# Attention scores: the lower half of the queries against 64 rows of keys, without a copy of that half

## The chip, the cores and the metric

The kernel runs on one core of a Trainium2 chip. The metric is the device time of one execution, in microseconds (us); the time given for a kernel is the median of its runs.

## What is computed

The reference is a trunk of two layers over 2048 tokens of width 1024. A layer normalises its input, multiplies it with `w_in` into eight sections, and runs two mixers beside each other: chunked softmax attention with 8 heads of width 64, and retention with 4 heads of width 128. Both are gated, joined, multiplied with `w_out` and added to the input. What the change touches is the attention's scores:

```python
qc = q.astype(jnp.float32).reshape(b, nc, CHUNK, h, dh)
...
kb = jnp.concatenate([kp[:, j:j + nc] for j in range(LEFT_CHUNKS + 1)], axis=2)
...
scores = jnp.einsum("bnqhd,bnkhd->bnhqk", qc, kb) * (dh ** -0.5)
...
scores = jnp.where(valid, scores + bias[None, None], NEG_INF)
p = jax.nn.softmax(scores, axis=-1)
```

A chunk of queries sees its own chunk of keys and the 8 before it.

## The kernel before, in words

All large products are made of f16 numbers that are split in two: an upper half (the f32 number rounded to f16) and a lower half (what is left, again in f16). A product of two split numbers takes three matmuls: upper by upper, upper by lower, lower by upper. The sums are kept in f32.

The work of a layer is tiled into four head groups (s), each with two attention heads and one retention head, and within a group into four stages (n) of 512 tokens. A stage has two dense parts and one attention part. `dense_T` (L654) makes queries, keys and the retention's rotated rows with channels on the partitions; `dense_V` (L785) makes values and gates with tokens on the partitions. `attention` (L823) works on the stage that was made before: 8 units of 128 queries and one head each, and beside it `retention` (L909). The order of the work on TensorE, ScalarE, VectorE and GpSimd is written out by hand as one program order: `run` (L1219) lets the dense generator go on for one round (8 matmuls of 512 columns as a rule), then gives the attention generator its turn, then some background work, while `later` (L637) puts small steps off by a number of rounds. A unit takes three rounds: `qk` (L830) with the scores in the first, the products with values (`pv`, L860) a unit or two later. The DMAs are issued from SyncE's queue (SP); those wrapped in `in_turn` keep their place in the program order, the others are placed by the framework's scheduler.

How the scores are stored and made before the change:

- In `evacuate(0)` (L673 to L689) the 512 query columns of both heads leave PSUM with 64 channels of each head on 64 partitions. ScalarE writes the upper half into `qq[:, 0]` (L677), one round later VectorE writes the lower half into `qq[:, 1]` (L680), and one round after that four DMAs (L687) copy both halves into `st.q`, so that for each head `hx` its 64 rows stand twice, on partitions 0 to 63 and again on 64 to 127.
- In `evacuate(1)` (L690 to L703) the keys go to `st.k[:, hx]`: 64 rows hold the upper half and the other 64 rows the lower half. For head 0 the upper half is on partitions 0 to 63, for head 1 on 64 to 127.
- In `qk` one matmul over 128 rows therefore makes q times the upper plus q times the lower half of the keys. The keys of a unit are up to 640 columns, cut into pieces (`cuts`, L840) where a new stage of keys or a new PSUM bank begins. Each piece gets two matmuls directly behind each other: the upper half of q (L845) and the lower half (L846). The 1184 products load their own weights, 128 columns of queries.
- VectorE adds the bias and takes the maximum (L849), ScalarE takes the exponential (L852) and its upper half (L854), GpSimd the lower half (L855), and a DMA transposes both (L857) for `pv` (L865 to L867).

Other lines that the prediction names: L778 and L797 are the dense products, L899 those of the retention, L1172 those of `w_out`. L581 and L587 belong to `rel_reverse` (L567), which turns the bias table round once at the start with small f32 products of 16 rows or 16 columns of weights; L272 are f32 transposes of the input, L761 dense products of the first stage, L1318 a product with ones that sums over partitions. The q copies of the first stage run before the first unit.

Of the kernel before, what the change touches and what calls it, by code (L numbers as in the profile page):

```python
# [8 lines left out]
F16 = mybir.dt.float16  # L9
# [3 lines left out]
AF = mybir.ActivationFunctionType  # L13
ALU = mybir.AluOpType
# [4 lines left out]
P = 128  # L19
# [8 lines left out]
def hybrid_trunk(ctx: ExitStack, tc: tile.TileContext, x, pos, gain, gcol, w_in, w_out, rel, fgain,  # L28
# [8 lines left out]
    act, dve, pool, pe, sp = nc.scalar, nc.vector, nc.gpsimd, nc.tensor, nc.sync  # L37
# [4 lines left out]
    b1 = ctx.enter_context(tc.tile_pool(name="b1", bufs=1))  # L42
    b2 = ctx.enter_context(tc.tile_pool(name="b2", bufs=2))
# [579 lines left out]
    def in_turn(i):  # L623

        if not ring.get("free"):
            return
        tc.keep_in_program_order(i)
# [9 lines left out]
    def later(k, fn):  # L637
        deferred.append([k, fn])
# [11 lines left out]
    def in_order(apart, terms):  # L650

        return [(kt, w) for w in terms for kt in range(KT)] if apart else [(kt, w) for kt in range(KT) for w in terms]

    def dense_T(l, s, n, g, st):  # L654
        hh, hl = hT[l, n]
        nm = f"{l}_{s}_{n}"
        st.tabc = b1.tile([P, 512], F32, tag="tabc", name=f"tabc{nm}")
        st.tabs = b1.tile([P, 512], F32, tag="tabs", name=f"tabs{nm}")
        def tab_load():
            while n not in tab_done:  # L660
                pull(1)
            in_turn(sp.dma_start(st.tabc, tab_d[n][0]))
            in_turn(sp.dma_start(st.tabs, tab_d[n][1]))

        first = (l, s, n) == (0, 0, 0)

        def soon(fn):
            if first:
                fn()
            else:  # L670
                later(1, fn)

        def evacuate(j, ps):  # L673
            if j == 0:
                st.q = b2.tile([P, 2, 2, 512], F16, tag="q", name=f"q{nm}")
                qq = b1.tile([P, 2, 512], F16, tag="qq", name=f"qq{nm}")
                act.activation(qq[:, 0, :], ps, AF.Copy, scale=2.0 ** -16)  # L677

                def q_rest():
                    dve.scalar_tensor_tensor(out=qq[:, 1, :], in0=ps, scalar=2.0 ** -16, in1=qq[:, 0, :], op0=ALU.mult,  # L680
                                             op1=ALU.subtract)
                    soon(q_copies)

                def q_copies():
                    for hx in range(2):
                        for half in range(2):
                            in_turn(sp.dma_start(st.q[half * 64:half * 64 + 64, hx], qq[hx * 64:hx * 64 + 64]))  # L687

                soon(q_rest)  # L689
            elif j == 1:  # L690
                st.k = b3.tile([P, 2, 512], F16, tag="k", name=f"k{nm}")
                kk = b1.tile([P, 2, 512], F16, tag="swp", name=f"kk{nm}")
                kh, kl = kk[:, 0, :], kk[:, 1, :]
                act.activation(kh, ps, AF.Copy, scale=2.0 ** -16)

                def k_rest():
                    dve.scalar_tensor_tensor(out=kl, in0=ps, scalar=2.0 ** -16, in1=kh, op0=ALU.mult, op1=ALU.subtract)  # L697
                    sp.dma_start(st.k[0:64, 0, :], kh[0:64, :])
                    sp.dma_start(st.k[64:128, 1, :], kh[64:128, :])
                    sp.dma_start(st.k[64:128, 0, :], kl[0:64, :])  # L700
                    sp.dma_start(st.k[0:64, 1, :], kl[64:128, :])

                soon(k_rest)  # L703
            else:
                w = 5 - j
                rot = b2.tile([P, w, 512], F16, tag=f"rot{j}", name=f"rot{nm}_{j}")
                if j == 2:
                    raw = rot[:, 1:3].rearrange("p a c -> p (a c)").bitcast(F32)
                else:
                    raw = b1.tile([P, 512], F32, tag="qq", name=f"raw{nm}")  # L710
                act.activation(raw, ps, AF.Copy, scale=2.0 ** -16)

                def swap(rot=rot, raw=raw, j=j):
                    swp = b1.tile([P, 512], F32, tag="swp", name=f"swp{nm}_{j}")
                    sp.dma_start(swp[0:64, :], raw[64:128, :])
                    sp.dma_start(swp[64:128, :], raw[0:64, :])

                    def turn():
                        pool.tensor_tensor(raw, raw, st.tabc, op=ALU.mult)  # L719
                        pool.tensor_tensor(swp, swp, st.tabs, op=ALU.mult)  # L720
                        pool.tensor_tensor(raw, raw, swp, op=ALU.add)  # L721

                    def upper():
                        act.activation(rot[:, 0], raw, AF.Copy)

                    def lower():
                        dve.tensor_tensor(rot[:, 1], raw, rot[:, 0], op=ALU.subtract)

                    def third():
                        act.activation(rot[:, 2], rot[:, 0], AF.Copy, scale=2.0 ** -11)  # L730

                    def tokens():
                        st.kt = b1.tile([P, KT, P], F16, tag="ktok", name=f"kt{nm}")
                        sp.dma_start_transpose(out=st.kt, in_=rot.rearrange("p a c -> p (a c)"))

                    if not first:
                        plan = {3: turn, 6: upper, 7: lower, **({9: third} if j == 2 else {10: tokens})}
                    elif j == 2:
                        plan = {4: turn, 11: upper, 12: lower, 13: third}
                    else:  # L740
                        plan = {3: turn, 5: upper, 6: lower, 7: tokens}
                    for k_, fn in plan.items():
                        later(k_, fn)

                if j == 2:
                    st.rq = rot
                    swap()
                    if first:
                        later(1, tab_load)
                else:  # L750
                    st.rk = rot
                    later(9 if first else 3, swap)

        if first:
            ps = [psD.tile([P, 512], F32, tag="dense", name=f"dT{nm}_{j}") for j in range(2)]
            for (j, a) in ((0, 0), (0, 1), (0, 2), (1, 0), (1, 1), (1, 2), (0, 3), (1, 3)):
                cs = slice(a * P, (a + 1) * P)
                m = 0
                for (w_, h_) in ((g.h, hh), (g.h, hl), (g.l, hh)):
                    for kt in range(KT):  # L760
                        pe.matmul(ps[j][:, cs], w_[:, j, kt, :], h_[:, kt, cs], start=(m == 0), stop=(m == 23))  # L761
                        m += 1
                yield
            for j in range(2):
                evacuate(j, ps[j])
                yield
        for j in range(2 if first else 0, 4):
            if j == 2 and not first:
                tab_load()
            if first:  # L770
                ps = psR.tile([P, 512], F32, tag="small", name=f"dT{nm}_{j}")
            else:
                ps = psD.tile([P, 512], F32, tag="dense", name=f"dT{nm}_{j}")
            while g.tdone <= j:
                pull(1)
            m = 0
            for kt, (w_, h_) in in_order(j == 0, ((g.h, hh), (g.l, hh), (g.h, hl))):
                pe.matmul(ps, w_[:, j, kt, :], h_[:, kt, :], start=(m == 0), stop=(m == 23))  # L778
                m += 1
                if m in (8, 16) or (m == 24 and first):  # L780
                    yield
            evacuate(j, ps)
            yield
# [39 lines left out]
    def attention(l, s, n, g, st, prev):  # L823
# [6 lines left out]
        def qk(a, hx):  # L830
# [7 lines left out]
            S = psS.tile([P, 1024], F32, tag="S", name=f"S{u.nm}")  # L838
            cs = slice(a * P, (a + 1) * P)
            cuts = sorted({0, nb} | {j for j in range(nb) if u.kts[j] == (st, 0) or j == 4})  # L840
            for j0, j1 in zip(cuts, cuts[1:]):
                q_, a_ = u.kts[j0]
                k_ = q_.k[:, hx, a_ * P:(a_ + j1 - j0) * P]
                o = S[:, j0 * P:j1 * P]
                pe.matmul(o, st.q[:, hx, 0, cs], k_, start=True, stop=False)  # L845
                pe.matmul(o, st.q[:, hx, 1, cs], k_, start=False, stop=True)  # L846
            v = b2.tile([P, 640], F32, tag="sc", name=f"sc{u.nm}")[:, 0:w]
            m = b2.tile([P, 1], F32, tag="mq", name=f"mq{u.nm}")
            dve.tensor_tensor_reduce(out=v, in0=S[:, 0:w], in1=g.bias[hx][:, 640 - w:640], scale=1.0, scalar=-3.0e38,  # L849
                                     op0=ALU.add, op1=ALU.max, accum_out=m)  # L850
# [505 lines left out]
    for j in range(4):  # L1356
        o = VSEC[j] * 512
# [80 lines left out]
    for l in range(DEPTH):  # L1438
        gO = [Grp(), Grp()]
        go = Grp()  # L1440
        for s in range(NSW):
            g = grp(l, s)
            for n in range(NS):
                first = (l, s, n) == (0, 0, 0)
                if not first:
                    st = St()
                    states[l, s, n] = st
                    dT = dense_T(l, s, n, g, st)
                else:
                    st = st0  # L1450
# [129 lines left out]
```

## Time and profile before

| what | value |
|---|---|
| median of 3 runs | 2060.21 us (2058.85 to 2062.08) |
| span of the profiled execution | 2060.7 us |
| TensorE products busy | 1999.4 us, 14038 products |
| weight loads busy | 1052.9 us, 14038 loads |
| VectorE, ScalarE, GpSimd busy | 1228.1, 1134.8, 688.1 us |
| mean granted TensorE clock | 0.995 |
| DMA | 313.64 MB, queue busy for 65.6% of 16 engines' span |

The span runs from the first to the last instruction of one profiled execution; the profile lists no time of its own for that execution, and its span lies within the range of the three runs. Engines are named PE (TensorE products), PEld (TensorE weight loads), DVE (VectorE), ACT (ScalarE), POOL (GpSimd) and SP. A row of a group reads: line, engine, operation, tiles written and read, for products the rows and columns of the weights (128*128), shapes, count, then busy time and mean length of one in ns, then the idle time ahead of it and what ended it. A row of the order of time reads: start, length, engine, line, operation, tiles, shapes, how many were merged. The ends of products are modelled and run past the start of the next product, so starts are what is to be compared.

### The profile page before, as it was taken

The numbers are of one execution on the slowest core, as the hardware profiler recorded it, in microseconds if no ns is written. First come the engines' busy times: TensorE is split into PE (matmuls) and PEld (weight loads), VectorE is DVE, ScalarE is ACT, GpSimd is POOL, SyncE is SP. The second block draws the span as 40 slices with busy tenths as digits, with TensorE's granted clock in tenths as the row PEclk, the third lists the DMA queues.
The fourth block names the chain that finished last, engine by engine and source line by source line (L and its number), as shares of the span: only waits on it lengthen the run. The fifth ranks groups of instructions, "written<-read, shape, count | busy, mean of one in ns | idle before, by whom it ended". The sixth has DMA issues, their size and how long they took to land. (4 is left out here: it accounts for less than half of the span.)

```text
span 2060.7 us, 39339 instructions
## 1 busy us (share of the span) xinstructions
PE 1999.4 (97%) x14038; PEld 1052.9 (51%) x14038; DVE 1228.1 (60%) x3804; ACT 1134.8 (55%) x2526; POOL 688.1 (33%) x701
## 2 busy tenths in 40 slices
PE   6988999999999999999999999999999999999998
PEld 4444555555555555554444555555555555555544
DVE  6776666565556555666553556555655566557643
ACT  6556665556565645555444546655656565455432
POOL 0344343434334434430003443444333334333100
PEclk9999999999999999999999999999999999999999
DMA  8778664547584754899774546554746775658864
GB/s 227 169 161 178 155 148 109 112 114 164 117 185 113 165 128 101 174 209 263 219 185 113 124 104 156 116 126 103 158 117 150 148 155 124 129 115 187 224 203 139
DMA packets 645701, 313.64 MB, mean 152 GB/s; under 512 B 459232, under 2 KB 602080, under 8 KB 645504
## 3 DMA queue, kind: packets, MB, share of 16 engines
q1 hardware_dynamic: 645504, 311.12, 65.6%
q8 instruction: 110, 1.80, 0.4%
q14 instruction: 87, 0.71, 0.1%
HBM read 123.26 MB, written 41.98 MB: 80 GB/s over the span
## 5 line engine op out<-in xcount | busy, mean ns | idle before, releaser
L855 POOL TENSOR_TENSOR pq<-sc,pq 128x640 f16<-128x640 f32 (+4 forms) x256 | 319.4, 1248 | 860.5 <-ACT pq L854 443.8
L852 ACT ACTIVATE sc<-sc,mq,cT 128x640 f32<-128x640 f32 (+4 forms) x256 | 218.4, 853 | 615.6 <-DVE rl L871 309.7
L797 PE MATMUL dV<-whV,hTh 128*128 128x512 f16 x1024 | 353.9, 381 | 7.3 <-DVE gt L815 6.1
L797 PE MATMUL dV<-whV,hTl 128*128 128x512 f16 x1024 | 353.8, 381 | 0.0
L797 PE MATMUL dV<-wlV,hTh 128*128 128x512 f16 x1024 | 353.8, 381 | 0.0
L778 PE MATMUL dT<-hTh,whT 128*128 128x512 f16 x1008 | 346.6, 379 | 2.7 <-DVE kk L697 1.3
L778 PE MATMUL dT<-hTl,whT 128*128 128x512 f16 x1008 | 346.6, 379 | 0.0
L778 PE MATMUL dT<-hTh,wlT 128*128 128x512 f16 x1008 | 346.6, 379 | 0.0
L797 PEld LDWEIGHTS <-hTh 128*128 128x128 f16 x2048 | 197.0, 98 | 224.7 <-DVE gt L815 10.0
L778 PEld LDWEIGHTS <-whT 128*128 128x128 f16 x2016 | 192.1, 98 | 207.7 <-issue 1.6
L849 DVE CUSTOM_DVE_ANT_0 sc<-S,bias 128x640 f32<-128x640 f32 (+4 forms) x256 | 188.3, 735 | 88.8 <-PE S L846 87.4
L1172 PE MATMUL dO<-whO,yly 128*128 128x512 f16 x504 | 191.0, 379 | 1.7 <-DMA yly<-hTl 1.1
L1172 PE MATMUL dO<-whO,yhy 128*128 128x512 f16 x504 | 191.0, 379 | 1.0 <-DMA yhy<-hTh 1.0
L1172 PE MATMUL dO<-wlO,yhy 128*128 128x512 f16 x504 | 191.0, 379 | 0.0
L854 ACT ACTIVATE pq<-sc 128x640 f16<-128x640 f32 (+4 forms) x256 | 171.5, 670 | 8.1
L797 PEld LDWEIGHTS <-hTl 128*128 128x128 f16 x1024 | 99.4, 98 | 112.4 <-issue 3.9
L1172 PEld LDWEIGHTS <-yhy 128*128 128x128 f16 x1008 | 98.1, 98 | 113.7 <-DMA yhy<-hTh 1.5
L778 PEld LDWEIGHTS <-wlT 128*128 128x128 f16 x1008 | 97.2, 98 | 113.7 <-issue 6.0
L845 PE MATMUL S<-k,q 128*128 128x128 f16 (+3 forms) x592 | 142.4, 267 | 0.0
L865 PE MATMUL o<-v,pT 128*128 128x65 f16 x1120 | 129.8, 193 | 6.4 <-DMA pT<-pq 5.5
L866 PE MATMUL o<-v,pT 128*128 128x64 f16 x1120 | 130.1, 195 | 0.0
L846 PE MATMUL S<-k,q 128*128 128x128 f16 (+3 forms) x592 | 129.7, 267 | 0.0
(359 smaller groups left out, 3476.5 us busy)
## 6 DMA issues: line engine op xcount, KB each, us to landing
q<-qq SPq DMA_DIRECT2D x128, 128.0 KB, 2.4
yyy<-y_d SPq DMA_DIRECT2D x32, 512.0 KB, 4.5
stT<-in_w_in_dram SPq DMA_DIRECT2D x27, 512.0 KB, 4.8
stV<-in_w_in_dram SPq DMA_DIRECT2D x26, 512.0 KB, 4.6
k<-kk SPq DMA_DIRECT2D x128, 64.0 KB, 2.0
swp<-rot SPq DMA_DIRECT2D x64, 128.0 KB, 3.1
tabc<-tab SPq DMA_DIRECT2D x32, 256.0 KB, 3.0
tabs<-tab SPq DMA_DIRECT2D x32, 256.0 KB, 3.1
```

Source lines behind the costliest of these rows:

```text
L778: pe.matmul(ps, w_[:, j, kt, :], h_[:, kt, :], start=(m == 0), stop=(m == 23))
L797: pe.matmul(ps, h_[:, kt, a * P:(a + 1) * P], w_[:, kt, :], start=(m == 0), stop=(m == 23))
L845: pe.matmul(o, st.q[:, hx, 0, cs], k_, start=True, stop=False)
L846: pe.matmul(o, st.q[:, hx, 1, cs], k_, start=False, stop=True)
L849: dve.tensor_tensor_reduce(out=v, in0=S[:, 0:w], in1=g.bias[hx][:, 640 - w:640], scale=1.0, scalar=-3.0e38, op0=ALU.add, op1=ALU.max, accu ...
L852: act.activation(v, v, AF.Exp, bias=m[:, 0:1], scale=g.c[:, 0:1])
L854: act.activation(pq[:, 0:w], v, AF.Copy)
L855: pool.tensor_tensor(pq[:, w:2 * w], v, pq[:, 0:w], op=ALU.subtract)
L865: pe.matmul(o[:, 0:65], u.p[:, b, :], v_[:, 0:65], start=(b == 0), stop=False)
L866: pe.matmul(o[:, 0:64], u.p[:, b, :], v_[:, 65:129], start=False, stop=False)
L1172: pe.matmul(ps, h_[:, kt, :], w_[:, kt, :], start=(m == 0), stop=(m == 23))
```

## The change

The lower half of q is no longer copied. `st.q` becomes `[P, 3, 512]`: parts 0 and 1 hold the upper half for head 0 and 1, each twice over the partitions as before; VectorE writes the lower half of both heads directly into part 2, where each head has its own 64 rows only. `qq` keeps the upper half alone, and each of the four copies moves one half instead of two. In `qk` all upper products of a unit are issued first, piece by piece, over 128 rows; then all lower products, over the 64 rows where that head's upper half of the keys stands. Products of the lower half of q with the lower half of k are thereby left out of the scores. The first product into a PSUM bank opens it, the last one into it closes it.

```diff
-                st.q = b2.tile([P, 2, 2, 512], F16, tag="q", name=f"q{nm}")
-                qq = b1.tile([P, 2, 512], F16, tag="qq", name=f"qq{nm}")
-                act.activation(qq[:, 0, :], ps, AF.Copy, scale=2.0 ** -16)
+                st.q = b2.tile([P, 3, 512], F16, tag="q", name=f"q{nm}")
+                qq = b1.tile([P, 512], F16, tag="qq", name=f"qq{nm}")
+                act.activation(qq, ps, AF.Copy, scale=2.0 ** -16)
...
-                    dve.scalar_tensor_tensor(out=qq[:, 1, :], in0=ps, scalar=2.0 ** -16, in1=qq[:, 0, :], op0=ALU.mult,
+                    dve.scalar_tensor_tensor(out=st.q[:, 2, :], in0=ps, scalar=2.0 ** -16, in1=qq, op0=ALU.mult,
                                              op1=ALU.subtract)
...
-                            in_turn(sp.dma_start(st.q[half * 64:half * 64 + 64, hx], qq[hx * 64:hx * 64 + 64]))
+                            in_turn(sp.dma_start(st.q[half * 64:half * 64 + 64, hx, :], qq[hx * 64:hx * 64 + 64, :]))
...
             cuts = sorted({0, nb} | {j for j in range(nb) if u.kts[j] == (st, 0) or j == 4})
+            rows = slice(hx * 64, hx * 64 + 64)
+            parts = []
             for j0, j1 in zip(cuts, cuts[1:]):
                 q_, a_ = u.kts[j0]
-                k_ = q_.k[:, hx, a_ * P:(a_ + j1 - j0) * P]
-                o = S[:, j0 * P:j1 * P]
-                pe.matmul(o, st.q[:, hx, 0, cs], k_, start=True, stop=False)
-                pe.matmul(o, st.q[:, hx, 1, cs], k_, start=False, stop=True)
+                parts.append((S[:, j0 * P:j1 * P], q_.k[:, hx, a_ * P:(a_ + j1 - j0) * P]))
+            opened = set()
+            for (j0, (o, k_)) in zip(cuts, parts):
+                pe.matmul(o, st.q[:, hx, cs], k_, start=j0 // 4 not in opened, stop=False)
+                opened.add(j0 // 4)
+            for i, (j0, (o, k_)) in enumerate(zip(cuts, parts)):
+                pe.matmul(o, st.q[rows, 2, cs], k_[rows], start=False,
+                          stop=i + 1 == len(parts) or cuts[i + 1] // 4 != j0 // 4)
```

In the changed kernel's numbering the upper products are L848 and the lower ones L851.

## Prediction

> **What bounds the kernel now.** I read the head of the page first, then the grouped rows, then the order of time inside one attention unit, and last the list of what TensorE waits for.
>
> ```profile
> span 2060.7 us, 39339 instructions
> ...
> PE 1999.4 (97%) x14038; PEld 1052.9 (51%) x14038; DVE 1228.1 (60%) x3804; ACT 1134.8 (55%) x2526; POOL 688.1 (33%) x701
> ...
> L849 DVE CUSTOM_DVE_ANT_0 sc<-S,bias 128x640 f32<-128x640 f32 (+4 forms) x256 | 188.3, 735 | 88.8 <-PE S L846 87.4
> ...
> L846 PE MATMUL S<-k,q 128*128 128x128 f16 (+3 forms) x592 | 129.7, 267 | 0.0
> ```
>
> TensorE is busy for 97% of the span, and no other engine passes 60%. The softmax row counts 256 units (a unit is 128 queries of one head). The score row counts 592 pieces, 592/256 = 2.3 to a unit, each with an upper product (L845) and a lower one (L846), and has no idle time before it. But a product's row runs on past the start of the next one, so what a product costs is the step from its start to the next start. That is read in the order of time (columns: start us, length us):
>
> ```profile
> 620.25 0.38 PE L846 MATMUL S<-k,q 128*128 128x512 f16 x1
> 620.47 0.22 PE L845 MATMUL S<-k,q 128*128 128x128 f16 x1
> 620.52 0.22 PE L846 MATMUL S<-k,q 128*128 128x128 f16 x1
> 620.58 0.38 PE L778 MATMUL dT<-hTl,whT 128*128 128x512 f16 x1
> ```
>
> Steps: 0.22 us for 512 columns, 0.055 us for 128, also from the unit into the dense product behind it. Only columns are paid for. The weight loads show why:
>
> ```profile
> 620.47 0.10 PEld L846 LDWEIGHTS <-q 128*128 128x128 f16 x1
> 620.52 0.15 PEld L778 LDWEIGHTS <-whT 128*128 128x128 f16 x2
> ```
>
> Each load begins with the product ahead of it (620.47, 620.52) and so lies beside that product. The kernel is bound by TensorE's stream, and time is lost or won where a step between starts grows or shrinks.
>
> **The change part by part.**
>
> *Columns: nothing.* The built program has the same 592 + 592 products over the same columns. The lower ones take weights of 64 rows by 128 columns, at row 0 or row 64 by head, in place of 128 by 128. The steps above go by columns, so I give half the rows no saving; the product of the two lower halves is left out of the scores without a gain in time.
>
> *Two changes of shape per unit: the cost.* A unit's products are regrouped: first all upper ones (128 rows), then all lower ones (64 rows), and behind them work on 128 rows again. That is 2 changes of the weights' shape in each of 256 units, 512 in all. The kernel before has four in the whole program, all in the preparation of rel_bias at 27 to 31 us, and they are the nearest rows there are. Merged rows of the products first (start, length of the whole row, count), then single ones, then the loads:
>
> ```profile
> 26.76 0.61 PE L761 MATMUL dT<-hTh,wlT 128*128 128x128 f16 x8
> 27.30 0.54 PE L581 MATMUL rlt<-ident,rl 16*128 16x16 f32 x6
> ...
> 28.29 1.07 PE L272 MATMUL ptn<-ident,xb 128*128 128x128 f32 x8
> 29.30 1.48 PE L587 MATMUL rlr<-anti,rt 128*16 128x128 f32 x12
> ...
> 27.63 0.21 PE L581 MATMUL rlt<-ident,rl 16*128 16x16 f32 x1
> ...
> 30.51 0.27 PE L587 MATMUL rlr<-anti,rt 128*16 128x128 f32 x1
> 30.71 0.23 PE L761 MATMUL dT<-hTh,whT 128*128 128x128 f16 x1
> ...
> 30.71 0.29 PE L761 MATMUL dT<-hTh,whT 128*128 128x128 f16 x2
> ```
> ```profile
> 27.30 0.44 PEld L581 LDWEIGHTS rlt<-ident,rl 16*128 16x128 f32 x6
> 27.77 0.10 PEld L1318 LDWEIGHTS <-ones 128*128 128x128 bf16 x1
> ...
> 29.29 1.20 PEld L587 LDWEIGHTS rlr<-anti,rt 128*16 128x16 f32 x12 [0.17 <-issue]
> 30.71 0.90 PEld L761 LDWEIGHTS <-whT 128*128 128x128 f16 x16 [0.21 <-ACT hTh L281]
> ```
>
> The last start in a merged row is its start plus its length, less the length of one product.
> - From 128*128 to 16*128 weights: last L761 start 26.76 + 0.61 - 0.22 = 27.15, next product 27.30. The step is 0.15, where these products step by (27.15 - 26.76)/7 = 0.055: 0.095 more. The load no longer begins with the product ahead (27.15) but at 27.30, with its own. I read it as the array being emptied first.
> - From 128*128 to 128*16: last L272 start 28.29 + 1.07 - 0.27 = 29.09, next 29.30. The step is 0.21, where the L587 products of the same 128 columns step by (30.51 - 29.30)/11 = 0.11: 0.10 more.
> - Out of 128*16: 30.51 to 30.71, 0.20 in place of 0.11: 0.09 more. The view puts the load's idle time down to ACT, yet the wait is as long as at the other changes.
> - Out of 16*128: the load stands 0.14 behind the last product (27.63 to 27.77); its product then waits for something else. So 0.14 is a bound only.
>
> The first product after a change has no load ahead of it, so the step behind it grows too: after 30.71 the second starts at 30.71 + 0.29 - 0.22 = 30.78, 0.07 in place of 0.055, some 0.01 more.
>
> Per change I take 0.095 + 0.01 = **0.105 us**, between ends of 0.09 and 0.14. No row has 64 rows of weights; the nearest is the first of the four, which also narrows the rows and keeps all columns. For in and out alike, 512 x 0.105 = **53.8 us** (ends 46.1 and 71.7), on the stream that nothing covers.
>
> The Trainium skill, TensorEngine Tiling (Array Packing), Key Properties, says that changing the tiling mode drains the engine, while another tile of the same mode does not; it gives no time. The Trainium skill's TensorE: Matmul & The Clock Gate, Part 2 (the step "DRAIN"), lets the last column leave after about 128 cycles, at 2.4 GHz an estimate from that page of 0.053 us per change, 27 us in all. The rows show nearly twice that, and they decide.
>
> *Stalls that take some of it up.* Where TensorE waits anyway, being later costs less. Of what it waits for from 80 us on (us in total, times, longest), the rows that matter here:
>
> ```profile
> PE r L899 <- DVE dT L907: 6.8, 9, 1.6
> PE o L865 <- DMA pT<-pq: 5.5, 9, 1.9
> ...
> PE dT L778 <- DMA hTh<-xa: 0.8, 1, 0.8
> ...
> PE dT L778 <- DVE qq L680: 0.6, 1, 0.6
> ```
>
> The first and the last are the ends of 15 rows with 37 stalls, 33.8 us. Each stall can hide at most its own length, and at most 2 x 0.105 = 0.21 us for each unit since the stall before; added up stall by stall that is an estimate of 12 us. But the chains that end in dT and pT begin with a product of TensorE and move with it. So 0 to 12, and I take a third: 4 us.
>
> *The copies: nothing on the path.* ScalarE's upper half and VectorE's rest (now written straight into the third part of q) keep their shapes and so their lengths. The built program shows no new wait for them: VectorE's rest even loses its waits for DMAs that read the old tile. On ScalarE, VectorE and GpSimd no instruction changes its place. On SP's queue a handful of issues trade places by one to five with their neighbours: five y_d stores, one load of output weights, one pair of table loads, the two transposes of one token tile. I price these at nothing: the stores have no reader before the output stage, GpSimd (33% busy) reads the tables, and the weights and the token tile are used a stage or more later; a late one would show as a new DMA stall of TensorE. The 128 copies go from 128 to 64 KB:
>
> ```profile
> q<-qq SPq DMA_DIRECT2D x128, 128.0 KB, 2.4
> ...
> k<-kk SPq DMA_DIRECT2D x128, 64.0 KB, 2.0
> ```
>
> By the k row they land 0.4 us sooner. No score product waits for them (idle 0.0). What lighter copies can give is the DMA stalls in layers where they run: 5.5 for pT and 0.8 for hTh, 6.3 us at most. I take 0, because a pT stall follows a chain over VectorE, ScalarE and GpSimd, and its transpose is only the last link.
>
> *Sum.* Against the profiled execution: 2060.7 + 53.8 - 4 = 2110.5 us of span. The median shown (2060.21) lies 0.5 below that span: **2110 us**, 2.4% more.
>
> **The rivals.**
>
> *No emptying at half height, and the lighter copies show (no change or faster).* The place is the step from upper to lower products and back. If 64 rows follow 128 as any other weights do, the time is 2060, and with all 6.3 us of DMA stalls gone 2054. It is faster only if a change of shape costs under 6.3/512 = 0.012 us. For it: no row shows 64 rows. Against it: three changes, in rows and in columns, in and out, read 0.09 or more. Chance 0.08, half of it within 0.2% (4 us, about what a measurement of this kernel can tell from no change) and half faster.
>
> *Loads that no longer lie beside products.* Then the 592 - 256 = 336 lower products that follow a lower one each wait for their load: 0.10 us as at 620.47, or 0.06 at the pace of the six L581 loads. That is 34 or 20 us more, 2130 to 2144. For it: the load of 16*128 at 27.30 did not lie beside the product ahead. Against it: that was only the first; the six products of L581 start within 0.33 us (27.30 to 27.63) with a load each, and the six loads end at 27.74, inside the last product's row. Chance 0.12. The Trainium skill, TensorE: Matmul & The Clock Gate, Part 3, states such a rule: a load overlaps a running product only where their row groups differ. The loads of full height at 620.47 and 620.52 already speak against it.
>
> *A cheap change* (0.05 us): 2060 + 26 = 2086. Against it are the same three readings. Chance 0.03.
>
> **How the numbers follow.** The forecast holds 0.77, with its own ends at 2060 + 46 - 12 = 2094 and 2060 + 72 = 2132. The range of 2094 to 2130 cuts little from it and takes in the edge of the load rival: about 8 in 10. Faster 0.04, same 0.04, slower 0.92 (0.77 + 0.12 + 0.03).
>
> **What would show it.** In the profile after: lower products with 64*128 weights; the step from the last upper product to the first lower one about 0.10 us over its columns, with its load beginning behind that product and not with it; the same from the last lower one to what follows; steps among the lower products by columns alone. TensorE's idle time should hardly grow, because rows of 0.22 us cover steps of 0.16; the span must show it. It would be wrong if the steps across the change stay at 0.055 (first rival), if lower products of 128 columns step by 0.09 or more among themselves (second), or if the span grows where no unit runs.

## The result, and the profile after

The changed kernel takes 2107.41 us (median, 2103.67 to 2107.71), the kernel before 2060.93 beside it: a ratio of 1.0221, 95% interval 1.0207 to 1.0236. It is 46.5 us slower; 2110 us was forecast. The profiled execution took 2107.59 us with a span of 2105.8 us.

The head of the page after, and the row of the softmax's first step:

```profile
span 2105.8 us, 39316 instructions
...
PE 2048.6 (97%) x14038; PEld 1038.7 (49%) x14038; DVE 1228.8 (58%) x3804; ACT 1137.4 (54%) x2526; POOL 690.5 (33%) x701
...
L855 DVE CUSTOM_DVE_ANT_0 sc<-S,bias 128x640 f32<-128x640 f32 (+4 forms) x256 | 188.6, 737 | 117.0 <-PE S L851 115.1
```

The number of products is the same, the busy time of the other engines too. VectorE now sits idle 28 us longer ahead of its softmax step (117.0 against 88.8), nearly all of it waiting for scores: they come later. The page cannot show why TensorE needs longer, because its busy time counts rows that run on past the next start. The groups kept apart by shape say what ran (mean length in ns behind the busy time), lower products first:

```profile
L851 PE MATMUL S<-k,q 64*128 64x128 f16 x304 | 58.6, 218 | 0.0
L848 PE MATMUL S<-k,q 128*128 128x128 f16 x304 | 58.6, 219 | 0.0
```

The rows' lengths are equal and there is no idle time. The order of time in one unit of two pieces shows it, products first, loads second:

```profile
628.08 0.43 PE L848 MATMUL S<-k,q 128*128 128x512 f16 x2
628.45 0.44 PE L851 MATMUL S<-k,q 64*128 64x512 f16 x2
628.82 0.34 PE L905 MATMUL r<-rot,rot 128*128 128x128 f16 x3
```
```profile
628.44 0.11 PEld L851 LDWEIGHTS <-q 64*128 64x128 f16 x2 [0.26 <-issue]
628.82 0.17 PEld L905 LDWEIGHTS <-rot 128*128 128x128 f16 x3 [0.26 <-issue]
```

The last upper product starts at 628.08 + 0.43 - 0.22 = 628.29, the first lower one at 628.45: 0.16 us for 128 columns, which step by 0.055 elsewhere. The last lower one starts at 628.45 + 0.44 - 0.22 = 628.67, the next product at 628.82: 0.15. Both times the load begins with its own product (628.44, 628.82) and not with the one ahead. It is the pattern of the early rows of the kernel before, now twice in every unit. Over all 512 changes of shape in this trace the load starts 4 or 5 ns ahead of its own product, and 0.09 to 0.10 us beyond the columns are spent ahead of both. That the array is being emptied in that time is a reading: the trace shows the wait, not what fills it.

Taken over all starts of products in both traces, the growth of the span divides like this (what a step takes for its columns alone is already taken off in the first four rows):

| where | us |
|---|---|
| from the last upper to the first lower product, 256 x 0.096 | 24.5 |
| from the last lower product to the next work, 255 x 0.095 (one ends in a stall) | 24.3 |
| the product behind that, 256 x 0.011 | 2.8 |
| the second lower product, 192 x 0.011 | 2.0 |
| less what the same steps of the kernel before take over their columns, mostly in stretches of half clock | -0.6 |
| units in all, with the one left out and rounding | 52.7 to 53.3 |
| stalls of TensorE from 80 us on (33.8 before, 28.7 after) | -5.1 |
| what remains, nearly all in stretches of half clock | -2.9 |
| span | 45 |

Two terms give time back. The stalls from 80 us on (us, times, longest):

```profile
PE o L871 <- DMA pT<-pq: 7.8, 7, 2.5
PE dV L797 <- DVE gt L815: 4.1, 3, 3.1
PE r L905 <- DVE sh L913: 3.6, 2, 2.1
PE r L905 <- DVE dT L913: 3.2, 7, 1.1
```

The wait for VectorE's dT fell from 6.8 to 3.2 us, as it would if VectorE, with 0.2 us more per unit, keeps up better; this was not tested by itself. The wait for the transposed pT rose from 5.5 to 7.8, so the lighter copies did not shorten it. The other term is the granted clock (1.00 is full). In the kernel before, then after (stretch, length, products busy, clock, DMA share and GB/s):

```profile
107.40:110.80 3.40, 3.30 (x14) 0.50 0.25 64
121.00:124.40 3.40, 3.23 (x14) 0.50 0.99 309
182.50:189.30 6.80, 5.78 (x31) 0.50 0.55 169
1609.20:1612.60 3.40, 3.40 (x20) 0.51 0.65 181
```
```profile
107.40:110.80 3.40, 3.10 (x25) 1.00 0.24 61
120.70:127.50 6.80, 6.13 (x21) 0.50 1.03 255
182.50:189.30 6.80, 3.75 (x30) 1.00 0.76 201
953.60:957.00 3.40, 3.40 (x10) 0.50 1.19 189
1609.20:1612.60 3.40, 3.40 (x25) 1.00 0.59 134
```

Between the start and the end of the work the kernel before has 17.0 us at half clock, the changed one 10.2. At half clock a step is twice as long (0.43 us for 512 columns at 184 us in the kernel before, 0.22 elsewhere), so 6.8 us less of it is worth up to 3.4 us; the steps say 2.9. The change did not cause this as far as the runs show: the profiled runs below that take as long as the kernel before have 13.7 to 20.5 us of half clock, and the one that takes as long as the changed kernel (the last piece alone over 64 rows) has 17.1. The longest stall of the kernel before (3.3 us, on VectorE's gt) ends at 183.5, inside such a stretch; what starts one was not tried.

### The profile page after: what moved, and what is told of

Same layout as the page of the kernel before. It is cut to its first block, busy times and chain, and to the rows that moved or that the text cites. A ratio compares the mean times of both kernels' runs of the same rounds, so it can differ in the third digit from the quotient of the medians.

```text
span 2105.8 us, 39316 instructions
## 1 busy us (share of the span) xinstructions
PE 2048.6 (97%) x14038; PEld 1038.7 (49%) x14038; DVE 1228.8 (58%) x3804; ACT 1137.4 (54%) x2526; POOL 690.5 (33%) x701
## 4 chain that ended last, share of the span: by engine, by line
PE 51%; DMA 2%; DVE 1%; ACT 1%; POOL 1%; issue 1%; SPq 1%; POOLq 0%; ACTq 0%
PE dO L1178 15%; PE dT L778 14%; PE dV L797 14%; PE r L905 2%; PE S L851 2%; PE S L848 1%; PE o L871 1%; PE o L872 1%; PE o L873 1%; DMA pT<-pq 1%; DMA swp<-rot 0%; DMA stO1m<-in_w_out_dram 0%; ACT sc L858 0%; POOL pq L861 0%; PE ptn L1051 0%
## 5 line engine op out<-in xcount | busy, mean ns | idle before, releaser
L855 DVE CUSTOM_DVE_ANT_0 sc<-S,bias 128x640 f32<-128x640 f32 (+4 forms) x256 | 188.6, 737 | 117.0 <-PE S L851 115.1
L871 PE MATMUL o<-v,pT 128*128 128x65 f16 x1120 | 129.1, 193 | 8.6 <-DMA pT<-pq 7.8
L873 PE MATMUL o<-v,pT 128*128 128x65 f16 x1120 | 128.6, 192 | 0.0
L958 POOL TENSOR_TENSOR rss<-rss,mhalf 128x1 f32<-128x1 f32 x128 | 77.1, 602 | 155.7 <-DVE rss L957 150.5
```

Source lines behind the costliest of these rows:

```text
L871: pe.matmul(o[:, 0:65], u.p[:, b, :], v_[:, 0:65], start=(b == 0), stop=False)
L873: pe.matmul(o[:, 0:65], u.p[:, u.nb + b, :], v_[:, 0:65], start=False, stop=(b == u.nb - 1))
L958: pool.tensor_tensor(ss, ss, mhalf, op=ALU.pow)
```

## The experiments

The theory: the cost is the number of times that the weights' shape changes between 128 and 64 rows (512 of them). Rivals: the products over 64 rows are slow in themselves; the regrouping costs; the data path (direct write, light copies, queue order) costs. Each run stands beside runs of the kernel before on the same chip. "The unit steps" are the steps between starts from a unit's first score product to the second product behind the unit, added up over all units without stalls; a change in them is against the kernel before.

### All products over 128 rows, with zeros

```diff
-                st.q = b2.tile([P, 3, 512], F16, tag="q", name=f"q{nm}")
+                st.q = b2.tile([P, 4, 512], F16, tag="q", name=f"q{nm}")
...
-                    dve.scalar_tensor_tensor(out=st.q[:, 2, :], in0=ps, scalar=2.0 ** -16, in1=qq, op0=ALU.mult,
-                                             op1=ALU.subtract)
+                    for hx in range(2):
+                        r, z = slice(hx * 64, hx * 64 + 64), slice(64 - hx * 64, 128 - hx * 64)
+                        pool.memset(st.q[z, 2 + hx, :], 0.0)
+                        dve.scalar_tensor_tensor(out=st.q[r, 2 + hx, :], in0=ps[r], scalar=2.0 ** -16, in1=qq[r],
+                                                 op0=ALU.mult, op1=ALU.subtract)
...
-                pe.matmul(o, st.q[rows, 2, cs], k_[rows], start=False,
+                pe.matmul(o, st.q[:, 2 + hx, cs], k_, start=False,
```

> The changed kernel with its grouping and its light copies, but each lower product runs over 128 rows again: the lower half of a head has a part of its own, with zeros in the other 64 rows, so the sums are those of the changed kernel (the product of the two lower halves stays out). It adds two GpSimd memsets and a second VectorE instruction per stage. Theory (the cost is the change of the weights' shape, 512 times): no change of shape is left in a unit, every step goes by columns, time back at 2061 (2055 to 2066). Rival (regrouping all upper ahead of all lower products, or the direct write by VectorE, is what costs): it stays near 2107. If the lighter copies are worth anything it would show here as under 2061, by at most 6.

Measured: 2066.11 us, ratio 1.0022 (1.0012 to 1.0032). The unit steps grew by 0.1 us in all, so the 53 us are gone with the shape. Left are 5 us over the kernel before, just past the top of what the theory gave; in the trace TensorE waits 59.1 us in all, 5.2 more than before. The last three experiments below look for them.

### Regrouping alone

```diff
+            parts = []
             for j0, j1 in zip(cuts, cuts[1:]):
...
-                o = S[:, j0 * P:j1 * P]
-                pe.matmul(o, st.q[:, hx, 0, cs], k_, start=True, stop=False)
-                pe.matmul(o, st.q[:, hx, 1, cs], k_, start=False, stop=True)
+                parts.append((S[:, j0 * P:j1 * P], k_))
+            opened = set()
+            for (j0, (o, k_)) in zip(cuts, parts):
+                pe.matmul(o, st.q[:, hx, 0, cs], k_, start=j0 // 4 not in opened, stop=False)
+                opened.add(j0 // 4)
+            for i, (j0, (o, k_)) in enumerate(zip(cuts, parts)):
+                pe.matmul(o, st.q[:, hx, 1, cs], k_, start=False,
+                          stop=i + 1 == len(parts) or cuts[i + 1] // 4 != j0 // 4)
```

> The kernel before with one part of the change alone: all upper products of a unit first, then all lower ones, all over 128 rows, with the double copy. Theory (change of shape): 2061 (2058 to 2064), steps by columns alone. Rival (grouping costs): 2107.

Measured: 2060.15 us, ratio 0.9997 (0.9988 to 1.0006), and 0.0 us of change in the unit steps. The regrouping is free, with its new order of opening and closing the PSUM banks, and that rival falls.

### More changes with the same products

The changed kernel with each lower product directly behind its upper one:

```diff
                 pe.matmul(o, st.q[:, hx, cs], k_, start=j0 // 4 not in opened, stop=False)
                 opened.add(j0 // 4)
-            for i, (j0, (o, k_)) in enumerate(zip(cuts, parts)):
+                i = cuts.index(j0)
                 pe.matmul(o, st.q[rows, 2, cs], k_[rows], start=False,
```

> The changed kernel with the 64-row products where the lower products stood before, each directly behind its upper one. The same 592 lower products of 64 rows, but 1184 changes of shape in place of 512. Theory (each change costs 0.096 us and the product behind it 0.011 more): 1184 x 0.107 = 127 us on the stream, less some 8 to 20 taken up by stalls, so 2168 to 2180. Rival (each product over 64 rows costs, whatever stands ahead of it): no different from 2107.

Measured: 2166.24 us, ratio 1.0510 (1.0495 to 1.0524). One unit of two pieces in its trace:

```profile
643.56 0.38 PE L848 MATMUL S<-k,q 128*128 128x512 f16 x1
643.87 0.39 PE L851 MATMUL S<-k,q 64*128 64x512 f16 x1
644.19 0.23 PE L848 MATMUL S<-k,q 128*128 128x128 f16 x1
644.35 0.23 PE L851 MATMUL S<-k,q 64*128 64x128 f16 x1
644.51 0.23 PE L905 MATMUL r<-rot,rot 128*128 128x128 f16 x1
```

The steps are 0.31, 0.32, 0.16 and 0.16 us in place of 0.22, 0.22, 0.055 and 0.055: 0.1 more at every one of four changes, in and out, behind long and short products. The unit steps grew by 123.3 us, which is 0.104 for each of 1184 changes; in the changed kernel it is 52.7/512 = 0.103. The time came out 2 us under the range that was forecast (2168 to 2180). The stalls gave back 16.0 us (53.9 in the kernel before, 37.9 here), within the 8 to 20 allowed for them; what was sized too high is the stream, 0.104 us for a change in place of 0.107.

### Fewer products over 64 rows, with the same changes

The first experiment with the last lower product of a unit alone over 64 rows:

```diff
-                pe.matmul(o, st.q[:, 2 + hx, cs], k_, start=False,
+                r_ = rows if i + 1 == len(parts) else slice(0, P)
+                pe.matmul(o, st.q[r_, 2 + hx, cs], k_[r_], start=False,
```

> The first experiment with the last lower product of each unit alone over 64 rows, the others over 128 rows with zeros: 256 products of 64 rows in place of 592, but still 512 changes of shape. Theory (changes): 256 x (0.096 + 0.095 + 0.011) = 52 us on the stream, less the 8 that the changed kernel's stalls and slow stretches gave back, so 2103 to 2107. Rival (products over 64 rows): 256/592 of 46.5, 2081.

Measured: 2107.94 us, ratio 1.0229 (1.0215 to 1.0243), with 52.9 us in the unit steps; the time lies 1 us above the range that was forecast (2103 to 2107) and far from the rival's 2081. 256 products over 64 rows cost as much as 592. So it is not their number that counts but that of the changes: this and the run before decide against the rival that 64 rows are slow in themselves.

### The same shape at other rows

```diff
-                pe.matmul(o, st.q[rows, 2, cs], k_[rows], start=False,
+                r_ = slice(64 - hx * 64, 128 - hx * 64) if j0 == 4 else rows
+                pe.matmul(o, st.q[r_, 2, cs], k_[r_], start=False,
```

> The changed kernel, but in the 240 units of five key tiles the last lower product (the one into the second PSUM bank) takes the other 64 rows of q and of the keys: the same 64x128 shape, another place. It computes something else than the scores' term there (the other head's lower half against this head's lower keys). Theory in its narrow form (a change of shape empties the array, a change of place within the shape does not): no step longer than by columns there, 2107, or down to 2094 if products in different rows run beside each other (240 x 0.055). Rival (any change of the rows in use empties the array): 240 x 0.107 = 26 us more on the stream, 2125 to 2133.

Measured: 2098.95 us, ratio 1.0183 (1.0169 to 1.0198). One unit, products and loads:

```profile
888.02 0.43 PE L848 MATMUL S<-k,q 128*128 128x512 f16 x2
888.39 0.39 PE L852 MATMUL S<-k,q 64*128 64x512 f16 x2
888.71 0.23 PE L906 MATMUL r<-rot,rot 128*128 128x128 f16 x1
```
```profile
888.39 0.10 PEld L852 LDWEIGHTS <-q 64*128 64x128 f16 x2 [0.26 <-issue]
```

Two lower products, 512 columns on the one half of the rows and 128 on the other, take 0.39 us together, where they take 0.44 in the changed kernel, and the next work starts 0.32 us after the first of them, not 0.37. Their starts lie 3 ns apart: they run side by side, into different PSUM banks. A change of place within the shape brings no wait, and the rival's 2125 to 2133 falls. In the units of three pieces the product over the other rows starts 6 to 8 ns behind the first lower product, before the second one, although it is issued last (in one unit 256, 128 and 256 columns start at 163.289, 163.296 and 163.409). The unit steps fell from 52.7 to 42.7 us. The units with such a product are 192 and not the 240 of the expectation (the other 64 have a single piece), and 192 x 0.056 = 10.8 us is about what fell away. So it is the shape, in the narrow form of the theory.

### One VectorE write and two more copies

The first experiment, with the lower half going through `qq` and two copies (lines against the changed kernel):

```diff
+                    for hx in range(2):
+                        pool.memset(st.q[64 - hx * 64:128 - hx * 64, 2 + hx, :], 0.0)
+                    dve.scalar_tensor_tensor(out=qq[:, 1, :], in0=ps, scalar=2.0 ** -16, in1=qq[:, 0, :], op0=ALU.mult,
+                                             op1=ALU.subtract)
...
+                        r = slice(hx * 64, hx * 64 + 64)
+                        in_turn(sp.dma_start(st.q[r, 2 + hx, :], qq[r, 1, :]))
```

> The first experiment again (all products over 128 rows, zeros in the other 64 rows), but VectorE writes the lower half in one instruction as in the kernel before, and two more copies of 64 KB per stage bring it to its rows; six copies of 64 KB stand where the kernel before has four of 128. If the 5 us of the first experiment came from the second VectorE instruction per stage: 2061 (2057 to 2063). If they came from the GpSimd memsets or from the tile's zeros: 2066 again. If lighter copies gain anything: under 2058.

Measured: 2064.02 us, ratio 1.0014 (1.0005 to 1.0023). That is between the two answers and its interval overlaps that of the first experiment: inconclusive. It takes VectorE's instruction away, but puts two more issues per stage into SP's queue.

### The slice of rows alone

The changed kernel with one edit:

```diff
-                pe.matmul(o, st.q[rows, 2, cs], k_[rows], start=False,
+                pe.matmul(o, st.q[:, 2, cs], k_, start=False,
```

> The changed kernel with one edit: the lower products take all 128 rows of the third part of q and of the keys, in place of the head's 64. In the other 64 rows that adds the other head's lower half times this head's lower keys, a term of the size of the one that the changed kernel leaves out. Copies, direct write, grouping and queue order are those of the changed kernel; only the shape differs. Theory: 2061 (2056 to 2064), so that the slice of rows alone is the whole difference. If the lighter copies are worth anything: under 2058, to 2054 at best. Rival (something in the data path costs as well, as the 3 to 5 us of the two runs with zero rows may hint): 2063 to 2066.

Measured: 2064.03 us, ratio 1.0010 (1.0001 to 1.0019), with -0.7 us in the unit steps. Two words of the slice are worth 43 us (2107.41 to 2064.03), and the -0.7 is half clock that fell into units of the kernel before. The time lies at the edge of the theory's range and inside the rival's (2063 to 2066), so a small cost in the data path is not excluded. What is left against the kernel before is 0.1%, between 0.2 and 4 us by the interval; the lighter copies and VectorE's lost waits gain nothing that shows. The wait for pT in this run, and VectorE's dT behind it:

```profile
PE o L871 <- DMA pT<-pq: 9.0, 7, 2.6
PE r L905 <- DVE dT L913: 7.8, 11, 1.6
```

Both are longer than before (5.5 and 6.8), with copies of half the size. In the first experiment, with the same copies, the wait for pT is 5.5, so what moves it stays open.

### Two memsets more

The run over full rows, with two GpSimd memsets per stage into a fourth part of `st.q` that nothing reads:

```diff
+                    for hx in range(2):
+                        pool.memset(st.q[hx * 64:hx * 64 + 64, 3, :], 0.0)
```

> The kernel of the run over full rows with two GpSimd memsets of 64x512 per stage into a part of q that nothing reads. If the memsets were what cost in the runs with zero rows: 3 to 5 us over the run over full rows. If not: the same time.

Measured: 2063.14 us, ratio 1.0006 (0.9996 to 1.0015). The memsets cost nothing that can be measured.

### Two VectorE writes in place of one

The run over full rows, with the write split:

```diff
-                    dve.scalar_tensor_tensor(out=st.q[:, 2, :], in0=ps, scalar=2.0 ** -16, in1=qq, op0=ALU.mult,
-                                             op1=ALU.subtract)
+                    for hx in range(2):
+                        r = slice(hx * 64, hx * 64 + 64)
+                        dve.scalar_tensor_tensor(out=st.q[r, 2, :], in0=ps[r], scalar=2.0 ** -16, in1=qq[r],
+                                                 op0=ALU.mult, op1=ALU.subtract)
```

> The kernel of the run over full rows with the lower half written in two VectorE instructions of 64 rows (0.69 us each) in place of one of 128. If VectorE's second instruction was what cost in the first run with zero rows: 3 to 5 us over the run over full rows. If not: the same time.

Measured: 2068.53 us, ratio 1.0027 (1.0016 to 1.0038), 4.5 us over the run over full rows (the intervals just meet). VectorE's rows for the write, in the kernel before and in this one, then what TensorE waits for in this one:

```profile
L680 DVE SCALAR_TENSOR_TENSOR qq<-dT,qq 128x512 f16<-128x512 f32 x32 | 21.9, 683 | 13.1 <-ACT qq L677 12.0 <-DMA pT<-pq 1.1
```
```profile
L682 DVE SCALAR_TENSOR_TENSOR q<-dT,qq 64x512 f16<-64x512 f32 x64 | 43.9, 686 | 13.9 <-ACT qq L677 13.4
```
```profile
PE o L873 <- DMA pT<-pq: 10.0, 8, 2.2
PE r L907 <- DVE dT L915: 8.4, 12, 1.6
```

64 partitions take as long as 128 (0.69 us), so the split adds 22 us to VectorE, and TensorE's waits in all are 63.2 us, against 52.6 in the run over full rows and 53.9 in the kernel before. (The profiled executions of the two runs lie 9 us apart, twice the distance of their medians.) This points to VectorE's second write for the 5 us of the first experiment; with intervals that meet, and an inconclusive run with one write, it is not shown.

No run was faster than the kernel before beyond the noise. The side-by-side products suggest one more form, not tried: the lower products of both heads together. The stream of the L846 products is about 61 us (304 x 0.055 + 112 x 0.109 + 112 x 0.163 + 64 x 0.216), half of it 30, against 256 changes at 0.103, 26 us. By this estimate the gain is 4 us at best, and it would need a second score tile in PSUM.

## Why the prediction was right

- *What bounds the kernel.* Right: the time moved with the steps of TensorE's stream and with little else.
- *Columns: nothing.* Right. Lower products of 64 rows step by 0.056, 0.109 and 0.162 us for 128, 256 and 384 columns, like those of 128 rows. Those of 512 columns always come first behind a change and step by 0.226 to the next lower one, the 0.011 included.
- *0.105 us per change, 53.8 us.* Right in mechanism and size: 0.103, and 53 us. The reading from four rows at the start, with 16 rows or 16 columns of weights, held for 64 rows. That the wait is the array being emptied was a reading in the prediction and stays one. The two ends (0.09 and 0.14) were wider than needed; the 0.14 behind the short products of L581 is not repeated anywhere.
- *Stalls take up 4 us.* A third of the bound, taken without a row for the third, and low: 5.1 us from stalls. Another 2.9 that the prediction did not have came from fewer stretches at half clock, which is chance of the profiled executions as far as the runs show. Together 8.0; the sum of span was 4.7 us too high (2110.5 against 2105.8).
- *Span and time.* The prediction took the time 0.5 us below the span. The changed kernel's profiled execution shows it 1.8 us above (2107.59 and 2105.8). The prediction set the span of one execution against the median of others. This mistake and the last one cancel in part, so that 2110 lies within 3 us of 2107.41 is partly luck.
- *The copies: nothing.* Right: in the run over full rows the copies land in 2.0 us as forecast and no time is won. VectorE's one write per stage into another tile cost nothing that can be told from noise either.
- *The rivals.* "No emptying at half height" falls with every step table. "Loads that no longer lie beside products" falls too: lower products that follow one another step by columns, 0.011 more for the step behind the first and 0.0 for later ones. The sentence of TensorE: Matmul & The Clock Gate, Part 3 (the Trainium skill), by which a load overlaps running products only where the row groups differ, is thus not what these traces show; the same part also lets a load for the background weight buffer go ahead, and no run here shows whether that is what happens. "A cheap change" at 0.05 us is half of the 0.095 measured. The 128 cycles of TensorE: Matmul & The Clock Gate, Part 2 (the Trainium skill), an estimate of 0.053 us, do not cover it. The rule of TensorEngine Tiling (Array Packing), Key Properties (the Trainium skill), agrees with the traces in both halves as far as the steps show it: a change of mode brings a wait (0.095 us), another tile of the same mode does not (3 ns between starts).

## What to carry to other kernels

On a kernel bound by TensorE's stream, a product over 64 rows that runs alone costs what one over 128 rows costs, and going from the one shape to the other and back costs 0.2 us here. A place in a trace where the shape changes, even one with 16 rows at the start, gave that price in its steps between starts, while busy and idle time hid it. If half the rows carry nothing, keep the full height with zeros or with a term too small to matter, or find enough products for both halves of the rows to run side by side.

## What the runs showed of the hardware that was not expected

- Products of the same 64x128 shape on different rows and into different banks start 3 ns apart and share their time: 512 and 128 columns in 0.32 us with the wait behind them, as 512 alone (0.319). One issued last of three started 6 to 8 ns behind the first, ahead of the second.
- The price of a change is nearly the same into and out of the 64-row shape: 0.096 us into it, and out of it 0.093 behind several lower products and 0.103 behind a single one, 0.095 on average. It is the same behind products of 128 and of 512 columns.
- Between the start and the end of the work, stretches at half clock come in lengths of 3.4 or 6.8 us in every run, 10.2 to 20.5 us in all, without regard to how long the run takes.
- A VectorE write over 64 partitions takes as long as over 128 (686 and 683 ns).
